# Two normalizations of a transformer block: the squares behind the second one taken as sums per 512 columns

## The chip, the cores and the metric

The program runs on one core of one Trainium2 chip. A core has TensorE (matmuls and transposes, with a separate path for its weights), VectorE, ScalarE, GpSimd (called POOL in the profile) and SyncE, whose queue issues most transfers. The metric is device time in microseconds (us) of one execution; lower is better.

## The reference, cut to what matters

Two transformer blocks in a row, for 256 rows of 2048 values, all in fp32. The first projects to attention and a gate, attends in a sliding window, projects back and adds the normalized result to x. The second has its scales, shifts and gates computed from a vector c, two attentions, an output projection and a feed-forward part. The change touches the two places where a projection ends, is normalized, is added to x, and the sum is normalized again for the next projection:

```python
def rmsnorm(x, g):
    xf = x.astype(jnp.float32)
    r = lax.rsqrt(jnp.mean(xf * xf, axis=-1, keepdims=True) + NORM_EPS)
    return (xf * r * g.astype(jnp.float32)).astype(x.dtype)
...
    y = (o * silu(z)) @ w_out            # first place
    x = x + rmsnorm(y, g_post)
    h = _rmsnorm(x, g_pre_mix) * (1.0 + sc1) + sh1
    proj = h @ w_in
...
    y = (sigmoid(ga) * ya + sigmoid(gb) * yb) @ w_o      # second place
    x = x + gt1 * _rmsnorm(y, g_post_mix)
    h = _rmsnorm(x, g_pre_ffn) * (1.0 + sc2) + sh2
    f = square(relu(h @ w_ff1)) @ w_ff2
```

## The kernel before, in words

The 256 rows are two halves t = 0 and 1 of 128 rows. A value that feeds a matmul is kept as a high part and a low remainder. A weight tile `rw` arrives by DMA, ScalarE copies its high part `wh` (L68) and VectorE takes the remainder `wl` (L69). A product is high x high, low x high (activation low) and high x low (weight low).

`unit` (L118 to L158) multiplies by 512 columns of a weight matrix, slice pair by slice pair: for each half 4 matmuls with `wh` (L75, L76) and 2 with `wl` (L78), all 512 columns wide. With `lag` the second half runs that many steps behind the first. Functions in the list `later` are called one step on. `blocks_of` (L160 to L183) computes 128 columns of a weight matrix for both halves together: 512-column matmuls with `wh` (L172), 256-column ones with `wl` (L174), by eight slices.

`project_and_norm` (L513) is called for both places. It runs four units of 512 columns, the last one with a lag of 7 steps. When a half of a unit is done, ScalarE squares it with a sum (L533) and VectorE multiplies it by the gain row (L538). Behind the last one the sums are added, POOL raises them to -1/2 (L216), VectorE forms xp = x + yn * r in four pieces (L549), ScalarE squares these (L550), the sums are added (L553), POOL gives the second factor, four pieces are scaled by it (L560, L562), TensorE transposes them (L565), ScalarE and VectorE apply scale and shift (L571, L574), and the result is split into the next operand's tiles (L195, L197), called A and B in the first place, B and D in the second.

`ada_rows` (L344) sends a row of the computed gates to HBM and back, spread over all partitions, by two transfers. It is put on a list of side work at L825. `out_b` (L838) is the last stage before the second place; its transposes go through `to_operand` (L203).

Every engine executes its own instructions in one fixed order, set when the program is built by the framework's scheduler, and waits on semaphores. SyncE's queue issues transfers in its order too, and an issue that waits holds up those behind it.

## Time and profile before

| | |
|---|---|
| time, median of 3 runs | 1794.07 us (1791.09 to 1795.02) |
| the profiled execution | 1789.49 us |
| its span | 1787.7 us |
| granted TensorE clock, mean | 0.998 |
| TensorE busy | 1769.1 us, 99% |
| VectorE busy | 1314.5 us, 74% |
| ScalarE busy | 859.6 us, 48% |
| mean DMA rate | 248 GB/s |

A timeline row gives the start, the time from there to the last end, and how many instructions it holds; the note in brackets is the idle time before the row and what ended it. Instructions of one engine overlap at their edges, so the pitch is read from the starts. Rows of one line may be joined (x8). For each of the 20 idle matmuls at the start (L236) the trace holds two records.

### The profile page before, as it was taken

What the parts mean: (1) busy time and instruction counts of PE and PEld (TensorE: products, weight loads), DVE (VectorE), ACT (ScalarE), POOL (GpSimd) and SP (SyncE); (2) the same over time, 40 slices, a digit from 0 to 9 for tenths busy, and PEclk for the clock granted to TensorE, in tenths of its full rate; (3) what the DMA queues carried; (4) which work ended last, traced back from release to release, by engine and by line L of the source; (5) the groups of instructions that cost most, each with busy time, mean ns of one, the idle gap of its engine ahead of it and who ended that gap; (6) DMA issues with size and microseconds to landing.
All of it is one profiled execution on the core that took longest, in us unless ns stands there. A gap on an engine that the chain in (4) does not pass through costs nothing.

```text
span 1787.7 us, 23509 instructions
## 1 busy us (share of the span) xinstructions
PE 1769.1 (99%) x8992; PEld 1495.5 (84%) x8992; DVE 1314.5 (74%) x1894; ACT 859.6 (48%) x1265; POOL 10.3 (1%) x16
## 2 busy tenths in 40 slices
PE   9999999999999999999999999999999999999998
PEld 8888888788888888888887878888888888888886
DVE  5998888668998897677777567767676756565656
ACT  6555454654454454444443466444344434344433
POOL 0000000000000000000000000000000000000000
PEclk9999999999999999999999999999999999999999
DMA  8887768754677775688786666766666655555552
GB/s 309 328 295 286 272 274 331 252 185 154 268 281 265 304 277 206 238 313 306 301 304 247 247 239 252 271 238 249 240 253 241 251 188 189 190 187 195 186 198 104
DMA packets 82192, 442.99 MB, mean 248 GB/s; under 512 B 9760, under 2 KB 9760, under 8 KB 43552
## 3 DMA queue, kind: packets, MB, share of 16 engines
q1 hardware_dynamic: 82080, 441.50, 67.3%
q8 instruction: 70, 1.15, 0.2%
q14 instruction: 42, 0.34, 0.1%
HBM read 435.14 MB, written 6.32 MB: 247 GB/s over the span
## 4 chain that ended last, share of the span: by engine, by line
PE 94%; DMA 2%; DVE 2%; ACT 1%; issue 0%; POOL 0%; SPq 0%; DVEq 0%; POOLq 0%; ACTq 0%
PE acc L172 22%; PE acc L75 19%; PE acc L78 18%; PE acc L76 18%; PE acc L174 11%; DMA xs<-in_x 1%; PE att L456 1%; PE tr L407 1%; PE att L764 1%; PE tr L446 1%; PE tr L724 1%; DMA rw<-in_win 0%; DMA rw<-in_wf 0%; PE tr L208 0%; PE tr L681 0%
## 5 line engine op out<-in xcount | busy, mean ns | idle before, releaser
L68 ACT ACTIVATE wh<-rw 128x1024 fp32r<-128x1024 f32 (+1 forms) x602 | 634.6, 1059 | 775.2 <-PE acc L76 473.3
L69 DVE TENSOR_TENSOR wl<-rw,wh 128x1024 fp32r<-128x1024 f32 (+1 forms) x602 | 731.4, 1220 | 341.6 <-ACT wh L68 334.6
L332 DVE SCALAR_TENSOR_TENSOR araw<-araw,aacc 128x1024 f32<-128x1024 f32 x176 | 213.8, 1218 | 52.3 <-DMA araw<-in_wada 52.0
L75 PE MATMUL acc<-wh,A 128*128 128x512 f32 x624 | 245.5, 393 | 0.4 <-ACT A L195 0.4
L76 PE MATMUL acc<-wh,A 128*128 128x512 f32 x624 | 243.4, 390 | 0.8 <-DVE A L197 0.8
L172 PE MATMUL acc<-B,wh 128*128 128x512 f32 x864 | 219.1, 395 | 0.0
L78 PE MATMUL acc<-wl,A 128*128 128x512 f32 x624 | 193.1, 390 | 0.0
L172 PEld LDWEIGHTS acc<-B,wh 128*128 128x128 f32 x864 | 155.7, 189 | 29.9 <-issue 1.3
L75 PE MATMUL acc<-wh,C 128*128 128x512 f32 x448 | 174.7, 390 | 1.6 <-ACT wh L68 1.6
L76 PE MATMUL acc<-wh,C 128*128 128x512 f32 x448 | 174.6, 390 | 0.0
L75 PEld LDWEIGHTS acc<-wh,A 128*128 128x128 f32 x624 | 117.2, 188 | 25.3 <-issue 1.0
L76 PEld LDWEIGHTS acc<-wh,A 128*128 128x128 f32 x624 | 117.3, 188 | 24.8 <-DVE A L197 1.2
L78 PEld LDWEIGHTS acc<-wl,A 128*128 128x128 f32 x624 | 117.0, 188 | 25.1 <-DVE wl L69 0.4
L78 PE MATMUL acc<-wl,C 128*128 128x512 f32 x448 | 137.9, 389 | 0.0
L75 PE MATMUL acc<-wh,B 128*128 128x512 f32 x320 | 126.3, 395 | 0.4 <-ACT B L195 0.4
L76 PE MATMUL acc<-wh,B 128*128 128x512 f32 x320 | 124.9, 390 | 0.8 <-DVE B L197 0.8
L174 PEld LDWEIGHTS acc<-B,wl 128*128 128x128 f32 x864 | 117.9, 190 | 8.5
L174 PE MATMUL acc<-B,wl 128*128 128x256 f32 x864 | 120.8, 282 | 0.0
L172 PE MATMUL acc<-D,wh 128*128 128x512 f32 x480 | 120.3, 392 | 0.0
L75 PEld LDWEIGHTS acc<-wh,C 128*128 128x128 f32 x448 | 84.1, 188 | 19.2 <-ACT wh L68 1.9
L172 PEld LDWEIGHTS acc<-D,wh 128*128 128x128 f32 x480 | 86.3, 189 | 15.4
L172 PE MATMUL acc<-A,wh 128*128 128x512 f32 x384 | 99.0, 399 | 0.0
(212 smaller groups left out, 1978.4 us busy)
## 6 DMA issues: line engine op xcount, KB each, us to landing
rw<-in_wf SPq DMA_DIRECT2D x124, 1024.0 KB, 4.8
araw<-in_wada SPq DMA_DIRECT2D x176, 512.0 KB, 5.8
rw<-in_win SPq DMA_DIRECT2D x40, 1024.0 KB, 5.5
rw<-in_wqk SPq DMA_DIRECT2D x32, 1024.0 KB, 4.8
rw<-in_wq SPq DMA_DIRECT2D x16, 1024.0 KB, 7.0
rw<-in_wout SPq DMA_DIRECT2D x16, 1024.0 KB, 5.8
rw<-in_wga SPq DMA_DIRECT2D x16, 1024.0 KB, 4.8
rw<-in_wgb SPq DMA_DIRECT2D x16, 1024.0 KB, 4.9
```

Source lines behind the costliest of these rows:

```text
L68: A.activation(wh, src, AF.Copy)
L69: V.tensor_tensor(wl, src, wh.bitcast(F32), op=ALU.subtract)
L75: PE.matmul(ps, lhs(ht, 0, k, t), wh[:, i], start=start and i == 0, stop=False)
L76: PE.matmul(ps, lhs(ht, 1, k, t), wh[:, i], start=False, stop=False)
L78: PE.matmul(ps, lhs(ht, 0, k, t), wl[:, i], start=False, stop=stop and i == len(ks) - 1)
L172: PE.matmul(ps, wh[:, kk], xs[kk].rearrange("p e t -> p (e t)"), start=first + kk == 0, stop=False)
L174: PE.matmul(ps[:, 0:T], wl[:, kk], xs[kk][:, 0], start=False, stop=first + kk == nk - 1)
L332: V.scalar_tensor_tensor(rw, rw, 0.5, cb, op0=ALU.mult, op1=ALU.mult, accum_out=cols[i][:, half, b:b + 1])
L407: PE.matmul(sps[e][:, i * nk:(i + 1) * nk], qT[64 * e:64 * e + 64, 2 * hf + i, t * 128:(t + 1) * 128], kTd[64 * e:64 * e + 64, g, 0:nk], s ...
L446: PE.transpose(tr[:, i * 128:(i + 1) * 128], s[:, h, b * 128:(b + 1) * 128], ident)
L456: PE.matmul(pos[t][:, hh * 64:(hh + 1) * 64], pT[:, i], vn[:, b, g * 64:(g + 1) * 64], start=b == 0, stop=b == nb - 1)
L724: PE.matmul(sp[:, i * nk:(i + 1) * nk], qT[:, h, t * 128:(t + 1) * 128], kT[:, h, 0:nk], start=True, stop=True)
```

## The change

- In `blocks_of` the low matmuls of all slices of a block come behind all of its high ones.
- `gpre` and the first weights are issued by ScalarE's queue, the latter in two pieces that are split one by one (`split_by_tile`). Eleven idle matmuls stand in front of the program, where 20 stood.
- `project_and_norm` takes three sums per 512 columns: of y squared, of (y times gain) squared, and of y times gain times x. x is loaded once more for it (`xq`). From them and the sum of x squared, kept in `msx`, the second factor is worked out with operations on one column; the sum x + yn * r is squared nowhere. For half 0 the four pieces of the operand are put off by 3 to 6 steps.
- The gate row of `ada_rows` is called behind `out_b`, by `soon(2, ...)`, and the last transposes of `out_b` one step later.

```diff
+    def split_by_tile(src, shape, pl):
+
+        wh = pl.tile(shape, F32R, name="wh")
+        wl = pl.tile(shape, F32R, name="wl")
+        for i in range(shape[1]):
+            A.activation(wh[:, i], src[:, i], AF.Copy)
+            V.tensor_tensor(wl[:, i], src[:, i], wh[:, i].bitcast(F32), op=ALU.subtract)
+        return wh, wl
...
+    def soon(n, f):
+
+        later.append(f if n == 0 else lambda: soon(n - 1, f))
...
-                if before:
-                    nc.sync.dma_start(rw[:, hh], src[:, hh])
+                if before and n == 0:
+                    for i in range(2):
+                        nc.scalar.dma_start(rw[:, i], src[:, i])
                     use()
-                parts.append(split(rw[:, hh], [128, 2, 512], "", split_pool()))
+                    parts.append(split_by_tile(rw[:, hh], [128, 2, 512], split_pool()))
+                else:
+                    if before:
+                        nc.sync.dma_start(rw[:, hh], src[:, hh])
+                        use()
+                    parts.append(split(rw[:, hh], [128, 2, 512], "", split_pool()))
...
+            if first == 0:
+                lows = []
             xs = [ht[(k0 + first + kk) // 8][:, (k0 + first + kk) % 8] for kk in range(8)]
             for kk in range(8):
                 PE.matmul(ps, wh[:, kk], xs[kk].rearrange("p e t -> p (e t)"), start=first + kk == 0, stop=False)
-            for kk in range(8):
-                PE.matmul(ps[:, 0:T], wl[:, kk], xs[kk][:, 0], start=False, stop=first + kk == nk - 1)
+                lows.append((wl[:, kk], xs[kk][:, 0]))
             if 8 * (hh + 1) % nk == 0:
+                for n, (wlk, xh) in enumerate(lows):
+                    PE.matmul(ps[:, 0:T], wlk, xh, start=False, stop=n == nk - 1)
...
-    for _ in range(20):
+    for _ in range(11):
...
-            nc.sync.dma_start(gpre, I["gpre"])
+
+            nc.scalar.dma_start(gpre, I["gpre"])
...
-        r = rstd(ss, f"x{t}")
+        V.tensor_scalar(msx[t], ss, 1.0 / D, EPS, op0=ALU.mult, op1=ALU.add)
+        r = power(msx[t], f"x{t}")
...
-            ssy = [pst.tile([128, 4], F32, name=f"ssy{t}") for t in range(2)]
+            sums = [pst.tile([128, 3, 4], F32, name=f"sums{t}") for t in range(2)]
+            tot = [pst.tile([128, 3], F32, name=f"tot{t}") for t in range(2)]
...
                     cc = slice(j * 512, (j + 1) * 512)
-                    A.activation(yn[t][:, cc], ps, AF.Square, accum_out=ssy[t][:, j:j + 1])
+                    sm = sums[t]
+                    xq = px.tile([128, 512], F32, name="xq", bufs=1)
+                    nc.sync.dma_start(xq, xsrc[t * 128:(t + 1) * 128, cc])
+                    A.activation(yn[t][:, cc], ps, AF.Square, accum_out=sm[:, 0, j:j + 1])
+                    V.tensor_tensor(yn[t][:, cc], ps, grow[:, cc], op=ALU.mult)
+                    A.activation(ps, yn[t][:, cc], AF.Square, accum_out=sm[:, 2, j:j + 1])
                     if j == 3:
-                        ss = pst.tile([128, 1], F32, name="ss")
-                        V.tensor_reduce(ss, ssy[t], axis=AX.X, op=ALU.add)
-                        r = rstd(ss, "y")
-                    V.tensor_tensor(yn[t][:, cc], ps, grow[:, cc], op=ALU.mult)
+
+                        m = pst.tile([128, 3], F32, name="m3")
+                        V.scalar_tensor_tensor(m[:, 0:1], sm[:, 0, 3:4], 1.0 / D, tot[t][:, 0:1], op0=ALU.mult,
+                                               op1=ALU.add)
+                        r = power(m[:, 0:1], "y")
+                    V.scalar_tensor_tensor(xq, yn[t][:, cc], 2.0, xq, op0=ALU.mult, op1=ALU.mult,
+                                           accum_out=sm[:, 1, j:j + 1])
+                    if j == 2:
+                        V.tensor_reduce(tot[t], sm[:, :, 0:3], axis=AX.X, op=ALU.add)
+                        V.tensor_scalar(tot[t], tot[t], 1.0 / D, None, op0=ALU.mult)
+                        V.tensor_scalar(tot[t][:, 0:1], tot[t][:, 0:1], EPS, None, op0=ALU.add)
                     if j == 3:
-                        finish(t, r)
-
-                def finish(t, r):
+                        V.scalar_tensor_tensor(m[:, 1:3], sm[:, 1:3, 3], 1.0 / D, tot[t][:, 1:3], op0=ALU.mult,
+                                               op1=ALU.add)
+                        V.scalar_tensor_tensor(m[:, 1:2], m[:, 2:3], r, m[:, 1:2], op0=ALU.mult, op1=ALU.add)
+                        V.scalar_tensor_tensor(msx[t], m[:, 1:2], r, msx[t], op0=ALU.mult, op1=ALU.add)
+                        V.tensor_scalar(msx[t], msx[t], EPS, None, op0=ALU.max)
+                        finish(t, r, power(msx[t], "h"))
+
+                def finish(t, r, r2):
                     rows = slice(t * 128, (t + 1) * 128)
-                    ss2 = pst.tile([128, 4], F32, name="ss2")
-                    for c in range(4):
+
+                    def operand(c):
                         cc = slice(c * 512, (c + 1) * 512)
-                        xp = px.tile([128, 512], F32, name="xp", bufs=4)
+                        xp = px.tile([128, 512], F32, name="xp", bufs=3)
                         nc.sync.dma_start(xp, xsrc[rows, cc])
-                        V.scalar_tensor_tensor(xp, yn[t][:, cc], r, xp, op0=ALU.mult, op1=ALU.add)
-                        A.activation(yn[t][:, cc], xp, AF.Square, accum_out=ss2[:, c:c + 1])
-                        xps.append(xp)
-                    ss = pst.tile([128, 1], F32, name="ss")
-                    V.tensor_reduce(ss, ss2, axis=AX.X, op=ALU.add)
-                    r = rstd(ss, "h")
-                    for c in range(4):
-                        xp = xps.pop(0)
-                        nc.sync.dma_start(xdst[rows, c * 512:(c + 1) * 512], xp)
-                        xn = yn[t][:, c * 512:(c + 1) * 512]
-                        if c == 3:
-                            A.activation(xn, xp, AF.Copy, scale=r)
+                        V.scalar_tensor_tensor(yn[t][:, cc], yn[t][:, cc], r, xp, op0=ALU.mult, op1=ALU.add)
+                        nc.sync.dma_start(xdst[rows, cc], yn[t][:, cc])
+                        xn = xp
+                        if c % 2:
+                            A.activation(xn, yn[t][:, cc], AF.Copy, scale=r2)
                         else:
-                            V.tensor_scalar(xn, xp, r, None, op0=ALU.mult)
+                            V.tensor_scalar(xn, yn[t][:, cc], r2, None, op0=ALU.mult)
...
+                    for c in range(4):
+                        if t == 0:
+                            soon(3 + c, lambda c=c: operand(c))
+                        else:
+                            operand(c)
...
-        side.append(ada_rows(2, gg1, first[:, 624:640], first[:, 640:656]))
...
-                later.append(lambda: to_operand(mT, 4 * j, t, o, 0.5))
+                soon(1 if j == 3 else 0, lambda: to_operand(mT, 4 * j, t, o, 0.5))
...
+        soon(2, lambda: drain([ada_rows(2, gg1, first[:, 624:640], first[:, 640:656])]))
```

On VectorE, behind the last Square of half 0 in the first place, before (`yr` and `hr` are the two factors, `xp` the pieces of the sum, `wl` the low parts of weights):

```order
330 L536 TENSOR_REDUCE ss<-ssy_2572 128x1
331 L538 TENSOR_TENSOR yn_2570<-acc,gpost 128x512
332 L215 TENSOR_SCALAR yv<-ss 128x1
333 L549 SCALAR_TENSOR_TENSOR xp<-yn_2570,yr,xp 128x512 x4
334 L69 TENSOR_TENSOR wl<-rw,wh 128x1024 x2
335 L553 TENSOR_REDUCE ss<-ss_3151 128x1
336 L215 TENSOR_SCALAR hv<-ss 128x1
337 L69 TENSOR_TENSOR wl<-rw,wh 128x1024
338 L562 TENSOR_SCALAR yn_2570<-xp,hr 128x512 x3
```

The same place now (`xq` is the extra load of x, `m` and `msx` one-column values):

```order
341 L594 SCALAR_TENSOR_TENSOR yn_2564<-yn_2564,yr,xp 128x512
342 L573 SCALAR_TENSOR_TENSOR xq,sums_2566<-yn_2564,xq 128x512
343 L594 SCALAR_TENSOR_TENSOR yn_2564<-yn_2564,yr,xp 128x512
344 L580 SCALAR_TENSOR_TENSOR m_3174<-sums_2566,tot_2568 128x2
345 L594 SCALAR_TENSOR_TENSOR yn_2564<-yn_2564,yr,xp 128x512
346 L582 SCALAR_TENSOR_TENSOR m_3174<-m_3174,yr 128x1
347 L69 TENSOR_TENSOR wl<-rw,wh 128x1024
348 L583 SCALAR_TENSOR_TENSOR msx_88<-m_3174,yr,msx_88 128x1
349 L69 TENSOR_TENSOR wl<-rw,wh 128x1024
350 L584 TENSOR_SCALAR msx_88<-msx_88 128x1
351 L69 TENSOR_TENSOR wl<-rw,wh 128x1024
352 L600 TENSOR_SCALAR xp<-yn_2564,hr 128x512 x2
```

The four pieces and a sum stood in front of two splits; now three pieces, the xy product and four small steps stand among three splits.

On TensorE, the transposes of half 0 in the first place and what follows them up to the next unit, before:

```order
859 L565 MATMUL tr<-first,yn_2570 128x128 x12
860 L75 MATMUL acc<-wh,D 128x512
861 L76 MATMUL acc<-wh,D 128x512
862 L78 MATMUL acc<-wl,D 128x512 x2
863 L75 MATMUL acc<-wh,D 128x512
864 L76 MATMUL acc<-wh,D 128x512
865 L75 MATMUL acc<-wh,D 128x512
866 L76 MATMUL acc<-wh,D 128x512
867 L78 MATMUL acc<-wl,D 128x512
868 L565 MATMUL tr<-first,yn_2570 128x128 x4
869 L78 MATMUL acc<-wl,D 128x512
870 L75 MATMUL acc<-wh,A 128x512
```

The same now (from the transposes to the next unit):

```order
857 L603 MATMUL tr<-first,xp 128x128 x8
858 L84 MATMUL acc<-wh,D 128x512
859 L85 MATMUL acc<-wh,D 128x512
860 L87 MATMUL acc<-wl,D 128x512 x2
861 L603 MATMUL tr<-first,xp 128x128 x4
862 L84 MATMUL acc<-wh,D 128x512
863 L85 MATMUL acc<-wh,D 128x512
864 L84 MATMUL acc<-wh,D 128x512
865 L85 MATMUL acc<-wh,D 128x512
866 L87 MATMUL acc<-wl,D 128x512 x2
867 L84 MATMUL acc<-wh,A 128x512
```

Eight transposes instead of twelve come first, and the four of the last piece no longer stand ahead of the next unit; in both orders 38 of the 48 matmuls of half 1 stand between half 0's last one and these transposes. Half 1's first transposes stand 40 matmuls into the next unit before, and 33 now.

On SyncE's queue, the gate row (`row`, `gg`) and the first weights of the second place (`in_wo`), before:

```order
283 L331 DMA araw<-in_wada 128x1024 x5
284 L352 DMA row_8443<-cols_323 128x16
285 L353 DMA gg_6801<-row_8443 128x2048
286 L135 DMA rw<-in_wo 128x2048 x8
287 L548 DMA xp<-xsave 128x512 x2
```

And now:

```order
291 L355 DMA araw<-in_wada 128x1024 x5
292 L376 DMA row_8548<-cols_319 128x16
293 L377 DMA gg_6821<-row_8548 128x2048
294 L144 DMA rw<-in_wo 128x2048 x4
295 L563 DMA xq<-xsave 128x512
```

The row stands where it stood, ahead of all weights of wo; the first load of `xq` has come behind the first four of these.

## Rows read from the trace of the kernel before

**Rows 1.** The page's line of engines: busy us, share of the span, instructions.
```profile
## 1 busy us (share of the span) xinstructions
PE 1769.1 (99%) x8992; PEld 1495.5 (84%) x8992; DVE 1314.5 (74%) x1894; ACT 859.6 (48%) x1265; POOL 10.3 (1%) x16
```

**Rows 2.** Waits of TensorE: us in total, times, longest us.
```profile
PE tr L565 <- DVE yn L562: 2.6, 4, 1.1
PE acc L75 <- ACT wh L68: 1.6, 1, 1.6
...
PE tr L208 <- DVE rw L849: 1.0, 2, 0.7
PE acc L76 <- DVE A L197: 0.8, 1, 0.8
PE acc L76 <- DVE B L197: 0.8, 1, 0.8
PE acc L75 <- ACT A L195: 0.4, 1, 0.4
PE acc L75 <- ACT B L195: 0.4, 1, 0.4
```

**Rows 3.** Timeline of TensorE, first blocks of ff1: start us, length, instruction, count.
```profile
1094.91 1.98 PE L172 MATMUL acc<-B,wh 128*128 128x512 f32 x8
1096.73 1.11 PE L174 MATMUL acc<-B,wl 128*128 128x256 f32 x8
...
1100.92 2.00 PE L172 MATMUL acc<-B,wh 128*128 128x512 f32 x8
1102.76 1.12 PE L174 MATMUL acc<-B,wl 128*128 128x256 f32 x8
```

**Rows 4.** Windows (busy by engine, then PEclk, DMA share, GB/s) and timeline, the start.
```profile
1.00:6.00 5.00, 4.92 (x23) 4.92 (x24) 0.91 (x3) 2.12 (x4) 0.00 (x0) 1.00 0.70 180
6.00:8.00 2.00, 2.00 (x16) 2.00 (x16) 0.00 (x0) 0.96 (x1) 0.00 (x0) 1.00 0.94 319
...
7.04 1.06 ACT L68 ACTIVATE wh<-rw 128x1024 fp32r<-128x1024 f32 x1 [2.29 <-DMA rw<-in_win]
...
8.28 0.48 PE L75 MATMUL acc<-wh,A 128*128 128x512 f32 x1
...
12.31 1.06 ACT L68 ACTIVATE wh<-rw 128x1024 fp32r<-128x1024 f32 x1 [0.34 <-DMA rw<-in_win]
...
14.12 0.39 PE L75 MATMUL acc<-wh,A 128*128 128x512 f32 x1
```

**Rows 5.** Timeline of TensorE, from out_b to the first matmul of wo.
```profile
975.42 0.63 PE L208 MATMUL tr<-first,rw 128*128 128x128 f32 x4 [0.73 <-DVE rw L849]
977.68 0.50 PE L75 MATMUL acc<-wh,C 128*128 128x512 f32 x1 [1.63 <-ACT wh L68]
```

**Rows 6.** Timeline of ScalarE, POOL, VectorE and TensorE, first place, half 0.
```profile
339.41 0.60 ACT L533 ACTIVATE yn<-acc 128x512 f32<-128x512 f32 x1 [4.49 <-PE acc L78]
...
341.02 0.55 POOL L216 TENSOR_TENSOR yr<-yv,mhalf 128x1 f32<-128x1 f32 x1 [293.14 <-DVE yv L215]
346.95 1.48 POOL L216 TENSOR_TENSOR hr<-hv,mhalf 128x1 f32<-128x1 f32 x1 [5.38 <-DVE hv L215]
...
341.61 2.74 DVE L549 SCALAR_TENSOR_TENSOR xp<-yn,yr,xp 128x512 f32<-128x512 f32 x4 [0.66 <-POOL yr L216]
344.27 2.35 DVE L69 TENSOR_TENSOR wl<-rw,wh 128x1024 fp32r<-128x1024 f32 x2
...
346.80 1.23 DVE L69 TENSOR_TENSOR wl<-rw,wh 128x1024 fp32r<-128x1024 f32 x1
348.47 1.28 DVE L562 TENSOR_SCALAR yn<-xp,hr 128x512 f32<-128x512 f32 x3 [0.44 <-POOL hr L216]
...
349.01 1.53 PE L565 MATMUL tr<-first,yn 128*128 128x128 f32 x12 [0.94 <-DVE yn L562]
...
355.08 0.50 PE L76 MATMUL acc<-wh,A 128*128 128x512 f32 x1 [0.85 <-DVE A L197]
```

**Rows 7.** Timeline of TensorE, first place, half 1.
```profile
364.53 1.53 PE L565 MATMUL tr<-first,yn 128*128 128x128 f32 x12 [0.24 <-DVE yn L562]
```

**Rows 8.** Timeline of TensorE, second place, half 0.
```profile
1064.07 1.50 PE L565 MATMUL tr<-first,yn 128*128 128x128 f32 x12 [1.10 <-DVE yn L562]
```

More of the change, by code (lines that the diff above doesn't have):

```diff
@@ L88, in step @@
                 gens.pop(0)
-    def flush():
-        while later:
-            later.pop(0)()
+    def soon(n, f):
+        later.append(f if n == 0 else lambda: soon(n - 1, f))
     def drain(gens):
@@ L213, in rstd, with power @@
         v = pst.tile([128, 1], F32, name=name + "v")
+        V.tensor_scalar(v, ss, 1.0 / D, EPS, op0=ALU.mult, op1=ALU.add)
+        return power(v, name)
+    def power(v, name):
         r = pst.tile([128, 1], F32, name=name + "r")
-        V.tensor_scalar(v, ss, 1.0 / D, EPS, op0=ALU.mult, op1=ALU.add)
         G.tensor_tensor(r, v, mhalf, op=ALU.pow)
@@ L232, in _build @@
     gpre = pc.tile([128, KT], F32, name="gpre")
+    msx = [pc.tile([128, 1], F32, name=f"msx{t}") for t in range(2)]
     idle = bank(patt, "att")
-    for _ in range(20):
+    for _ in range(11):
         PE.matmul(idle[:, 0:128], ones, ones, start=True, stop=True)
@@ L576, in finish @@
                         evict_split(out, 4 * c, t, tmp, 4)
-                xps = []
+                    for c in range(4):
[3 more added lines that the diff above has]
+                            operand(c)
                 unit(w, j, ht, done, lag=LAG if j == 3 else 0, rate=0.67 if first and j < 3 else 0.0)
```

## The prediction

> **What bounds the kernel now.** I read the page's engine line first [rows 1]: TensorE has work in flight for 1769.1 of the 1787.7 us span, 99%, and no other engine passes 84%. So a change can move the end only by changing how many matmul columns pass or how close they stand, or by opening or closing TensorE's gaps. Second, the waits of TensorE [rows 2]: the longest kinds are its waits in front of the transposes of the second normalization (2.6 us over the four chains, two halves in each of two places), the evictions behind them (0.8 + 0.8 + 0.4 + 0.4), and one place around out_b (1.0 and 1.6). The reader is to see how little there is: the normalizations hold 5.0 us of idle time and the out_b place 2.6, with some 0.2 us more lost at each restart. Third, the timelines of those stretches, engine by engine, walked by hand below. Sums are made against the profiled execution (1789.49 us, span 1787.7); it lies 4.6 us under the median of the three runs, 1794.07, and the difference found is carried over to that median.
>
> **Pass order.** 108 blocks have 16 weight slices. Before, each does 8 high matmuls, 8 low, 8 high, 8 low; now 16 high and then 16 low. The work is the same; only the change from 256-column to 512-column matmuls becomes rarer. Eight high matmuls take 1.82 us to the next instruction where a 512-column matmul stands in front (1094.91 to 1096.73) and 1.84 where a low one does (1100.92 to 1102.76) [rows 3]. So one such change fewer is worth about 0.02 us per block, 108 x 0.018 = 1.9 us: **-1.9 us**, between 0 and -3. The low weights are held one half longer, but nothing waits for those buffers in [rows 2].
>
> **First transfers.** The gpre columns and the first weights (now two pieces) are issued by ScalarE's queue instead of SyncE's, the split works by piece, and 11 idle matmuls stand in front instead of 20. Before, the idle ones run without a break until the first weights are split (7.04 + 1.06 = 8.10) and the first real matmul starts at 8.28 [rows 4]. The piecewise split can bring that forward by about half a split, 0.5 us. But the third pair of slices is split at 12.31 + 1.06 = 13.37 and wanted at 14.12: a start more than 0.75 us earlier only meets that transfer. I take **-0.4 us**. Bounds: -1.5 if the later transfers come forward too; +1.5 if TensorE's clock is low when the real work starts. For the idle records run at two paces, 23 in the 5 us before 6.0 and 16 in the 2 us behind (granted clock shown as 1.00 in both), so 11 instructions, 22 records, end near 5.9 and leave a gap of 1 to 2 us that was not there.
> The Trainium skill (DMA: Bandwidth & Descriptors, Issuing engines are not separate DMA queues) says that transfers from several engines end up on the same 16 DMA engines and only the issuing time is saved. The DMA share of 0.70 and 0.94 in those two stretches does not contradict it; by that rule the first weights, issued later than before and sharing with the second pair, would land no sooner, and the term would be 0.
>
> **Gate row.** The source now calls the row's assembly after out_b and puts the last transposes one step later. On SyncE's queue the two row transfers still stand ahead of the first weights of wo, and on TensorE the eight transposes still stand in one piece ahead of the first matmul of wo. The 1.63 us wait for that first split stays [rows 5]: **0 us**; bounds 0 and -2.6 (the idle time there).
>
> **The second normalization.** Per 512 columns and half there is one more transfer of 256 KB, one more Square on ScalarE and one more product with a sum on VectorE. For the first three of the four column groups they lie beside a TensorE that does not wait for them. VectorE is 74% busy and ScalarE 48% [rows 1]. I cost them at nothing; without that cover they would be 12 times some 0.7 us on VectorE. What counts is the last group, where the chain from the last Square to the transposes is on the path.
> Before, with T = 339.41, the start of the last Square of half 0 in the first place [rows 6]: the first xp product starts at T + 2.20 behind POOL's power, the four take 2.66, two weight splits and the sums follow, a third split starts at T + 7.39, and POOL's second power runs beside it from T + 7.54 to T + 9.02. The scale starts at T + 9.06, the transposes at T + 9.60 after a wait of 0.94, and the second matmul of the next unit at T + 15.67.
> Now, walked in VectorE's new order: product at T + 2.1; then two xp products, the xy product and a third xp product, 4 x 0.665 = 2.66, with two one-column operations of 0.15, to T + 5.1; then a split of 1.17, a one-column step of 0.17, a second split, a second step: T + 7.8. The power starts at T + 8.0, again beside a split, and takes 1.48: T + 9.5, and the scale begins at **T + 9.7**, 0.6 us later than before, not earlier. The four Squares and the sum that left the chain paid for themselves before by lying on ScalarE beside the two splits; in their place stand two short steps, each behind a whole split.
> TensorE has the same 38 matmuls to cover this as before, so it arrives at the same T + 8.45 and waits 1.8 us instead of 1.1 (idle 0.94 and the restart). Then comes the eviction of the next operand: same work, starting later, with only three of the four transposed groups of half 0 done; the next unit starts near T + 16.1 with a second stall of 2.0 (before: 0.4 + 0.85 and two restarts, 1.8). For half 1 I see more loss. Before, 40 matmuls of the next unit stand between the start and its transposes, which then wait only 0.24 [rows 7]; now 33 do, 1.6 us less cover, while its scale comes only some 0.6 us sooner: a stall of 1.1. Three matmuls behind it comes half 1's operand, which has to be evicted first: 1.6; and 0.4 at the last group. Together 1.8 + 2.0 + 1.1 + 1.6 + 0.4 = 6.9 against 1.1 + 1.8 + 0.3 = 3.2: **+3.7 us**.
> The second place is walked the same way: there the first wait is 1.10 [rows 8], the sum before 3.3 and after 6.9, **+3.6 us**. I give each place 1.5 us either way; the ends are -3.2 (no wait left) and +6.
> POOL's power takes 0.55 us where VectorE rests and 1.48 beside a weight split [rows 6]. If the second power met a resting VectorE, each of the first two stalls would be 0.9 shorter, and the time 1797.3; I take 1.48, since a split stands right behind the last one-column step in the new order too.
> The Trainium skill (SBUF — State Buffer, SBUF: two separate sides) says why the order decides it: a VectorE instruction with two SBUF inputs and a GpSimd one that reads SBUF lock each other out for their whole length, whichever starts first. By that rule a power that starts ahead of the split would take 0.55 and hold the split up instead; the trace of before shows only the other case, 1.48.
>
> **Sum.** -1.9 - 0.4 + 0 + 3.7 + 3.6 = +5.0 us: 1794.5 for the profiled execution, 1794.07 + 5.0 = **1799.1** against the median.
>
> **Rivals.**
> *The chain gets shorter, as the source has it.* Four Squares (some 2.5 us) are gone from it; the one-column steps may slip in while splits wait for their high parts, and only two scaled groups are needed before transposes begin. For: splits on VectorE do wait for ScalarE in other stretches, since every split stands behind its high part. Against: three splits stand in the new order inside the chain. If the idle time of both places shrinks by half, -3, the sum is -1.9 - 0.4 - 3 = -5.3, 1788.8. It decides where the second power starts before T + 6.5. This is the case on the faster side. Chance 0.19.
> *The normalizations come out as before.* The lost cover and the shorter chain cancel: only pass order and start count, -2.3, 1791.8. For: the waits of before are short, and TensorE does the same work between the same two ends. Chance 0.24.
> *The start loses.* In the gap behind 11 idle matmuls TensorE falls back to the pace that it had in the first 5 us, 0.217 against 0.125 us a record [rows 4]; some 20 real matmuls that take 1.7 times as long (0.40 instead of 0.23) cost 3.4 us, of which the wait for the third pair hides about half, on top of the forecast: 1801. Chance 0.09.
> *The gate row does move*, and the 2.6 us go: with the forecast elsewhere 1796.5, no change. Chance 0.03.
> The forecast has 0.45.
>
> **How the numbers follow.** About 0.2%, 3.6 us, is what a measurement can tell from no change: 1790.5 to 1797.7. Faster: the first rival, and a small part of the second, 0.21. The same: most of the second, the fourth and the low end of the forecast (1.5 us either way at each place), 0.31. Slower: the rest of the forecast and the third, 0.48. The forecast's own range is 1796 to 1802; with the second rival and the edge of the first, and the start's +1.5, the range is 1789 to 1802.5.
>
> **What would show it.** Right: in the profile after, TensorE's idle time ahead of the first transposes of each normalization near 1.6, four stalls in each instead of three, and a second power that starts about 8 us behind the last Square beside a weight split. Pass order: two halves of a block 5.57 us apart instead of 5.58. Gate row: still a wait of 1.6 ahead of wo. Start: first real matmul near 7.8, the third pair at about 14. Wrong: a power that ends under 8 us behind the Square, or transposes that wait less than 0.5 us, sends it to the first rival; matmuls 0.4 us apart in the first 12 us, to the third.

## The result, and the profile after

The changed kernel takes 1801.69 us (median of 4 runs, 1801.30 to 1804.87), the kernel before 1793.30 on the same chip (4 runs): the ratio is 1.0051 with a 95% interval of 1.0038 to 1.0064, so it is slower by about 9 us. The forecast was slower, by 5.0, at 1799.1.

The profiled execution took 1801.44 us and its span is 1799.7, 12.0 more than the one of before. That pair lies further apart than the medians, 8.4. The page of the changed kernel, its line of engines (busy us, share, instructions), against [rows 1]:

```profile
PE 1772.8 (99%) x8974; PEld 1496.5 (83%) x8974; DVE 1326.0 (74%) x1939; ACT 868.4 (48%) x1270; POOL 10.3 (1%) x16
```

VectorE and ScalarE have 12 and 9 us more work, and neither is short of time: the loss must be gaps of TensorE or a slower pace. Its waits, the same view as [rows 2] (us in total, times, longest us):

```profile
PE tr L603 <- DVE xp L600: 4.8, 3, 3.1
PE acc L84 <- ACT wh L77: 1.9, 2, 1.5
PE acc L87 <- DVE wl L69: 1.9, 2, 1.5
PE acc L84 <- ACT A L213: 1.7, 2, 0.9
PE acc L84 <- ACT wh L68: 1.6, 1, 1.6
PE acc L84 <- ACT B L213: 1.6, 1, 1.6
...
PE acc L85 <- DVE A L215: 1.1, 2, 0.8
PE tr L226 <- DVE rw L892: 1.0, 2, 0.7
PE tr L226 <- DVE cols L373: 0.7, 1, 0.7
PE tr L226 <- DVE mix L892: 0.4, 1, 0.4
PE acc L85 <- DVE B L215: 0.2, 1, 0.2
```

The waits at the second normalization's transposes went from 2.6 to 4.8 with one of 3.1, the evictions behind them from 2.4 to 4.6 (L213 and L215 together), and new are the waits for the first weights (L77), for a low part of weights (L69) and, around out_b, for `cols` and `mix` (1.1 together). L226 <- rw and L84 <- wh L68, around the gate row, read as before.

To see where the time goes, each instruction of TensorE is paired with the same one of before, and the start times are subtracted. The difference, by the time in the kernel before, with those of the experiments told of below:

```
us later than before at  100    325    345    384    450    480    700    970   1050   1165   1775
changed kernel           1.2    1.2    1.9    5.5    6.1    7.8    7.7    9.2   10.7   12.9   12.0
pass order alone         0.5    0.6    0.6    0.6    0.7    2.5    2.3    7.8    7.8    7.6    6.7
first transfers alone    1.7    2.4    2.4    2.4    2.4    2.5    2.5    2.5    2.5    2.5    2.5
normalization alone      0.0    0.3    5.9   12.7   13.2   13.2   13.3   14.1   16.9   18.0   18.0
gate row alone          -0.4   -0.4   -0.4   -0.4   -0.3   -0.3   -0.3    7.8    9.4    9.5    9.5
```

The steps of the first row: start 1.2, first place 4.9 (325 to 450), index stage 1.7 (450 to 480), at the transposes of out_b 1.5 (700 to 970), a low pace behind the gate row 1.5 (970 to 1050), second place 2.2 (1050 to 1165), and the feed-forward blocks behind it give 0.9. Not all of these belong to the change: the gate row alone left every engine's order as it was, and yet it lost 8.1 us between 700 and 970, from nothing but the scatter of one execution to the next. 30 executions of the kernel before on one chip ran from 1789.4 to 1800.7 us. So a step behind 700 us in one trace alone is not yet put down to the change; steps ahead of it are read from the traces.

The start of the changed kernel, TensorE's timeline (start, length, instruction, count, idle before), against [rows 4]:

```profile
1.08 5.06 PE L259 MATMUL att<-ones 128*128 128x128 f32 x22 [1.08 <-DVE ones L249]
7.63 0.80 PE L84 MATMUL acc<-wh,A 128*128 128x512 f32 x1 [1.48 <-ACT wh L77]
...
9.73 0.80 PE L84 MATMUL acc<-wh,A 128*128 128x512 f32 x1 [0.46 <-ACT wh L77]
...
11.61 0.63 PE L85 MATMUL acc<-wh,A 128*128 128x512 f32 x1
12.03 0.63 PE L84 MATMUL acc<-wh,A 128*128 128x512 f32 x1
```

The first real matmul starts 0.65 us sooner than the 8.28 of before, but its fellows stand 0.42 us apart (11.61 to 12.03) up to 13.7, and the second piece of the weights is late: ScalarE splits it at 9.05. At 20 us TensorE is 2.4 us late; half of that comes back at 48 us, where the kernel before itself waits 1.00 us for ScalarE (`qn`) and the changed one does not.

The first place: the gain product of the kernel before, which [rows 6] leaves out, then ScalarE and VectorE of the changed kernel, the same view:

```profile
340.21 0.68 DVE L538 TENSOR_TENSOR yn<-acc,gpost 128x512 f32<-128x512 f32 x1
```

```profile
341.29 0.60 ACT L564 ACTIVATE yn<-acc 128x512 f32<-128x512 f32 x1 [3.00 <-PE acc L87]
```

```profile
340.71 1.23 DVE L356 SCALAR_TENSOR_TENSOR A<-A 128x1024 f32<-128x1024 f32 x1 [0.49 <-DMA A<-in_wada]
...
342.33 1.22 DVE L356 SCALAR_TENSOR_TENSOR A<-A 128x1024 f32<-128x1024 f32 x1
...
344.13 0.68 DVE L565 TENSOR_TENSOR yn<-acc,gpost 128x512 f32<-128x512 f32 x1
...
345.55 0.75 DVE L594 SCALAR_TENSOR_TENSOR yn<-yn,yr,xp 128x512 f32<-128x512 f32 x1 [0.66 <-POOL yr L237]
...
352.48 0.88 DVE L600 TENSOR_SCALAR xp<-yn,hr 128x512 f32<-128x512 f32 x2 [0.44 <-POOL hr L237]
```

The last Square starts at T = 341.29. The gain product starts at T + 2.84, where it was T + 0.8 in before: two column sums of the scales (L356) and what hangs on them stand ahead of it. From there to the scaling it takes 8.35 us (344.13 to 352.48), just what it took before, 8.26 from the gain product at 340.21 to 348.47. The scale begins at T + 11.2; I had said T + 9.7. What put the column sums there is on SyncE's queue, the changed kernel's timeline (start of the issue, its length):

```profile
335.14 0.33 SPq L563 DMA_DIRECT2D xq<-in_x  x1
335.51 0.90 SPq L355 DMA_DIRECT2D A<-in_wada  x2
336.51 0.38 SPq L144 DMA_DIRECT2D rw<-in_win  x1
340.25 0.33 SPq L563 DMA_DIRECT2D xq<-in_x  x1
```

`xq` has one buffer. The load at 335.14 could be issued only when the product of the group before had read the buffer (to 335.1), and the one at 340.25 likewise (340.2). The last weights of the column sums and those of the next unit stood behind it in the queue's order; in before the last of these column weights were issued at 304 us.

The second place, TensorE of the changed kernel, against [rows 8]:

```profile
1073.41 0.63 PE L603 MATMUL tr<-first,xp 128*128 128x128 f32 x4 [1.14 <-DVE xp L600]
...
1087.51 1.53 PE L603 MATMUL tr<-first,xp 128*128 128x128 f32 x12 [0.63 <-DVE xp L600]
1090.63 0.49 PE L84 MATMUL acc<-wh,B 128*128 128x512 f32 x1 [1.59 <-ACT B L213]
1091.36 0.50 PE L85 MATMUL acc<-wh,B 128*128 128x512 f32 x1 [0.23 <-DVE B L215]
```

There half 0 waits as before (1.14 against 1.10) and no longer for its operand; half 1 waits 0.63 + 1.59 + 0.23, where it had 0.33.

### The profile page after: what moved, and what is told of

Its sections match the earlier page's. It is cut to its first block, busy times and chain, and to the rows that moved or that the text cites. A ratio compares the mean times of both kernels' runs of the same rounds, so it can differ in the third digit from the quotient of the medians.

```text
span 1799.7 us, 23545 instructions
## 1 busy us (share of the span) xinstructions
PE 1772.8 (99%) x8974; PEld 1496.5 (83%) x8974; DVE 1326.0 (74%) x1939; ACT 868.4 (48%) x1270; POOL 10.3 (1%) x16
## 4 chain that ended last, share of the span: by engine, by line
PE 92%; DVE 5%; DMA 1%; ACT 1%; issue 1%; POOL 0%; DVEq 0%; POOLq 0%; ACTq 0%; SPq 0%
PE acc L189 21%; PE acc L84 18%; PE acc L85 18%; PE acc L87 18%; PE acc L193 11%; DVE wl L69 1%; PE att L481 1%; DMA rw<-in_win 1%; PE tr L432 1%; DVE sc L736 1%; PE att L808 1%; PE tr L471 1%; PE tr L768 1%; PE tr L226 0%; ACT wh L68 0%
## 5 line engine op out<-in xcount | busy, mean ns | idle before, releaser
L68 ACT ACTIVATE wh<-rw 128x1024 fp32r<-128x1024 f32 (+1 forms) x601 | 633.7, 1058 | 684.3 <-PE acc L85 455.4
L69 DVE TENSOR_TENSOR wl<-rw,wh 128x1024 fp32r<-128x1024 f32 (+1 forms) x601 | 725.8, 1222 | 298.5 <-ACT wh L68 232.3
L84 PE MATMUL acc<-wh,A 128*128 128x512 f32 x624 | 247.2, 396 | 3.6 <-ACT wh L77 1.9
L356 DVE SCALAR_TENSOR_TENSOR araw<-araw,aacc 128x1024 f32<-128x1024 f32 x176 | 213.7, 1220 | 36.3 <-DMA araw<-in_wada 36.0
L84 PE MATMUL acc<-wh,C 128*128 128x512 f32 x448 | 175.5, 392 | 1.6 <-ACT wh L68 1.6
L84 PEld LDWEIGHTS acc<-wh,A 128*128 128x128 f32 x624 | 117.9, 189 | 30.0 <-ACT wh L77 3.0
L84 PE MATMUL acc<-wh,B 128*128 128x512 f32 x320 | 127.1, 397 | 1.6 <-ACT B L213 1.6
L189 PEld LDWEIGHTS acc<-D,wh 128*128 128x128 f32 x480 | 90.1, 188 | 18.6
L84 PEld LDWEIGHTS acc<-wh,C 128*128 128x128 f32 x448 | 84.5, 189 | 19.3 <-ACT wh L68 1.9
L87 PE MATMUL acc<-wl,B 128*128 128x512 f32 x320 | 99.3, 392 | 0.0
```

The source lines that it names most:

```text
L68: A.activation(wh, src, AF.Copy)
L69: V.tensor_tensor(wl, src, wh.bitcast(F32), op=ALU.subtract)
L84: PE.matmul(ps, lhs(ht, 0, k, t), wh[:, i], start=start and i == 0, stop=False)
L87: PE.matmul(ps, lhs(ht, 0, k, t), wl[:, i], start=False, stop=stop and i == len(ks) - 1)
L189: PE.matmul(ps, wh[:, kk], xs[kk].rearrange("p e t -> p (e t)"), start=first + kk == 0, stop=False)
L356: V.scalar_tensor_tensor(rw, rw, 0.5, cb, op0=ALU.mult, op1=ALU.mult, accum_out=cols[i][:, half, b:b + 1])
```

## The experiments

Twelve kernels, each built from the kernel before. A ratio is to runs of the kernel before on the same chip, with its 95% interval.

**Pass order alone.** The edit of `blocks_of` in the diff above, nothing else.

> Before with the pass order alone (all 16 high matmuls of a block, then all 16 low). Theory A, read from the two traces: the blocks save 0.26 us over the first 16, some 0.4 over the next 32 and 1.1 over the last 60, 1.7 in all, but the scheduler, which plans VectorE's order anew, puts one weight split behind the key rotation of the index stage (L786) instead of ahead of it, and TensorE waits 1.7 us for it near 470 us, as in the changed kernel: 1793.3 - 1.7 + 1.7 = 1793.3, within 1 us of before, and the trace shows that one wait. Rival B, my forecast's term: the saving alone, 1791.4, with no such wait.

1.0006 (0.9993 to 1.0019). Theory A; rival B's 1791.4 us would be 0.9988, outside the interval. The new wait is there, one of TensorE's waits in that kernel:

```profile
PE acc L78 <- DVE wl L69: 1.5, 1, 1.5
```

By the table it costs 1.8 us (450 to 480), and the 60 last blocks give 1.1 (1050 to 1775). The order on VectorE shows the cause: before, the weight split stands ahead of the chain of `rb`, `rl` and `kT` in the index stage, with pass order alone behind it:

```profile
465.97 1.21 DVE L69 TENSOR_TENSOR wl<-rw,wh 128x1024 fp32r<-128x1024 f32 x1
...
471.55 0.68 DVE L783 TENSOR_TENSOR kT<-rl,rb 128x512 f32<-128x512 f32 x1
```

```profile
471.11 0.68 DVE L786 TENSOR_TENSOR kT<-rl,rb 128x512 f32<-128x512 f32 x1
...
472.10 1.22 DVE L69 TENSOR_TENSOR wl<-rw,wh 128x1024 fp32r<-128x1024 f32 x1
```

In the changed kernel too: `kT` at 476.43 and the split at 477.42, with TensorE waiting.

**First transfers alone**, and **the same with 20 idle matmuls**:

```diff
-    for _ in range(11):
+    for _ in range(20):
```

> Before with the new first transfers and 11 idle matmuls alone. Theory A: the matmuls from 7.6 to 13.7 us run 0.43 us apart instead of 0.23, and the sequence behind them is 1.5 us late, as in the changed kernel: 1794.8. Rival B, my forecast's term: the start is 0.4 us sooner, 1792.9, and what the changed kernel loses there comes from elsewhere.

> Before with the new first transfers, but 20 idle matmuls as before. Theory A (the start loses by TensorE's pace, not by the transfers): the idle ones bridge the time to the first weights, the real matmuls stand 0.23 us apart from the start, and the sequence at 50 us is at most 0.5 us later than before, where with 11 idle ones it was 2 us later: 1793.7. Rival B (the transfers themselves came later, since the second piece of the first weights lands behind the second pair): still 2 us later, 1795.

1.0006 (0.9993 to 1.0019) with 11 and 0.9999 (0.9983 to 1.0015) with 20: no time can tell them from before or from each other, so the trace has to speak. At 100 us they are 1.7 and 1.6 us late. So rival B: 20 idle matmuls do not mend it. Their kernel's timeline:

```profile
8.44 0.50 PE L84 MATMUL acc<-wh,A 128*128 128x512 f32 x1 [1.04 <-ACT wh L77]
8.78 0.40 PE L85 MATMUL acc<-wh,A 128*128 128x512 f32 x1
10.15 0.50 PE L84 MATMUL acc<-wh,A 128*128 128x512 f32 x1 [0.98 <-ACT wh L77]
...
11.58 0.63 PE L85 MATMUL acc<-wh,A 128*128 128x512 f32 x1
12.01 0.63 PE L84 MATMUL acc<-wh,A 128*128 128x512 f32 x1
```

TensorE starts at the high pace (0.34 us from 8.44, with the first one's restart in it) and waits again for the second piece, which puts it 1.3 us behind before; the pace falls at 11.2, behind these two waits of 1 us, and costs 1.5 us more, until at 48 us some 1.2 come back as above. So the transfers lose time without any help of the pace; that the waits bring the pace down is what the order of the two suggests, no run separates them. The Trainium skill (DMA: Bandwidth & Descriptors, Issuing engines are not separate DMA queues) says that transfers which several engines start run on the same 16 DMA engines, and that only the time of the issue is saved. The trace agrees: the first weights are split at 7.04 in before, their two pieces at 6.95 and 9.05 in the changed kernel and at 7.77 and 9.47 with 20 idle matmuls.

**Gate row alone.**

> Before with the gate row behind out_b and the later last transposes alone. The program's instructions stand in the order of before on every engine, so any theory expects 1793.3 us, 0 within 0.2%. What differs between the two traces is then what one and the same program does from one execution to the next: by theory A the waits at 972 to 974 us and the low clock behind 987 us, 2.9 us in the changed kernel's trace, may show here too, by rival B (these belong to the change) never.

1.0004 (0.9989 to 1.0019), with the same order of instructions on every engine: the part does nothing. Its profile holds a wait that the one of before does not have, on VectorE and then on TensorE:

```profile
873.82 1.23 DVE L332 SCALAR_TENSOR_TENSOR araw<-araw,aacc 128x1024 f32<-128x1024 f32 x1 [6.24 <-DMA araw<-in_wada]
```

```profile
878.79 0.63 PE L208 MATMUL tr<-first,mix 128*128 128x128 f32 x4 [3.21 <-DVE mix L848]
```

A late transfer of the side work (issued at 863.72, landed at 873.72; the one before it took 6.3 us) stops VectorE for 6.2 us, and a product of the main work stands behind it; TensorE then runs at a granted clock of 0.50 from 881 to 886 us. So the waits at 970 us and the low pace behind 985, 3.0 us of the 12.0 between the profiled executions, are of a kind that the program of before shows by itself (rival B falls); whether the change makes them more frequent these runs can't tell.

**Normalization alone.**

> Before with the three sums and the deferred operand alone (the second normalization). Theory A: the first place loses 4.7 us (VectorE's column sums of the scales, whose last weights land late, stand ahead of the last gain product, so that the whole chain starts 2 us late and TensorE waits 3 us at the transposes), the second place 1 us in waits, and 1.8 more if TensorE's clock falls behind them: 1793.3 + 5.7 to 7.5 = 1799 to 1801, with the wait of 3 us in the trace. Rival B, my forecast: 3.7 and 3.6 us, 1800.6, with waits of 1.8 at the transposes in both places and no late start of the chain.

1.0038 (1.0019 to 1.0057), 1801.06 us: by the medians nearly the whole loss of the changed kernel. In its profile, of the slowest of its seven executions (1807.38 us), the loss is larger, and begins sooner than theory A has it, in front of the last unit: 5.6 us between 325 and 345. ScalarE and VectorE of that kernel:

```profile
333.45 1.06 ACT L68 ACTIVATE wh<-rw 128x1024 fp32r<-128x1024 f32 x1 [3.81 <-DMA rw<-in_wout]
```

```profile
318.00 0.69 DVE L553 SCALAR_TENSOR_TENSOR xq<-yn,xq 128x512 f32<-128x512 f32 x1 [2.42 <-DMA xq<-in_x]
```

It is the single buffer again, by another way. The load of `xq` is issued at 311.58, when its buffer is free, and lands at 317.90; a load of the projection's own weights stands behind it in the queue (312.00, where before has 305.82). VectorE waits 2.42 us for `xq` ahead of two weight splits, and the next loads of weights wait for buffers that the splits free: they are issued at 321.00 and 325.70, where before has 316.71 and 322.14, and the last one lands at 333.43 instead of 326.91.

**Column sums earlier; no deferral; xq on another queue.** Three edits of the normalization alone, one each (`...` stands for arguments left as they are):

```diff
-                unit(..., rate=0.67 if first and j < 3 else 0.0)
+                unit(..., rate=0.8 if first and j < 3 else 0.0)
```
```diff
-                        if t == 0:
-                            soon(3 + c, lambda c=c: operand(c))
-                        else:
-                            operand(c)
+                        operand(c)
```
```diff
-                    nc.sync.dma_start(xq, ...)
+                    nc.scalar.dma_start(xq, ...)
```

> The kernel with the normalization change alone, its side work in the first place (the last columns of the scales) paced at 0.8 instead of 0.67. By the order of its instructions the column sums are then done before the last gain product of half 0, and the chain behind that product has two weight splits in it instead of three. Theory A (the first place loses because these column sums, whose weights land late, stand ahead of the chain): the wait at the first transposes there falls from 1.8 to 3 us to under 1, the place loses 2 us or less instead of 4 to 7, and the time is 1797. Rival B (the lost cover behind half 1 and the evictions decide, as in my forecast): 1800, with the waits in front of half 1's operand unchanged.

> The kernel with the normalization change alone, but the pieces of half 0's operand are not put off. By its order twelve transposes come first again, as in before, and the fourth piece comes ahead of the next unit. Theory A (late column sums and the queue): the wait at the first transposes stays near 3, since the chain ahead of it is the same, and the time stays within 2 us of the 1800 of the normalization alone. Rival B (the deferral lost the cover): half 1's operand no longer waits, 1.5 us in each place come back, 1797.

> The kernel with the normalization change alone, the extra load of x (xq) issued by ScalarE's queue instead of SyncE's. Theory A (xq has one buffer, its issue waits for the product of the group before, and the weights of the scales and of the next units stand behind it on SyncE's queue): with xq off that queue the last weights of the scales are issued near 304 to 310 us as in before, not at 335, the splits do not wait for weights, and the first place loses 2 us or less: 1796 to 1797. It can lose on ScalarE, where the issue now waits in front of weight splits: each such wait over 1 us would show as a wait of TensorE for wh. Rival B (the chain itself, not the queue): 1800.

1.0041 (1.0027 to 1.0056), 1.0042 (1.0026 to 1.0058) and 1.0058 (1.0040 to 1.0075): none helps, the last is if anything worse. Theory A falls in the first: the column sums are out of the way, and the wait at the transposes is longer, 4.3 us. VectorE and TensorE of that kernel:

```profile
345.76 0.69 DVE L553 SCALAR_TENSOR_TENSOR xq<-yn,xq 128x512 f32<-128x512 f32 x1 [2.24 <-DMA xq<-in_x]
```

```profile
352.09 1.12 PE L583 MATMUL tr<-first,xp 128*128 128x128 f32 x4 [4.29 <-DVE xp L580]
```

Behind the column sums had hidden what now comes first: the x of the last group is issued when its buffer is free (341.27), lands 4.4 us later, and VectorE waits 2.24 us for it in the middle of the chain. On ScalarE's queue it is the same, 2.37 us: the queue is not what makes this load late, the single buffer is. There the last column weights are issued at 304 to 307 us again, as in before, so it was `xq` on SyncE's queue that had moved them; but that alone gives no time back. Without the deferral the waits for half 1's operand are gone, as rival B has it, but half 1's transposes in the second place wait 2.43 us, and 6.6 us go between 325 and 345 us as in the profile of the normalization alone.

**One ring of four buffers.**

```diff
-                    xq = px.tile([128, 512], F32, name="xq", bufs=1)
+                    xq = px.tile([128, 512], F32, name="xp", bufs=4)
...
-                        xp = px.tile([128, 512], F32, name="xp", bufs=3)
+                        xp = px.tile([128, 512], F32, name="xp", bufs=4)
```

> The kernel with the normalization change alone, but the extra load of x takes its buffer from the four that the pieces xp had before (one ring of 4, instead of 1 for xq and 3 for xp). Theory C, formed from the two runs before: xq has one buffer, so the last group's x is issued only behind the product of the group before, some 4.5 us late, and VectorE waits 2.2 to 2.4 us for it in the middle of the chain; the weights of the scales stand behind that issue as well. With the ring this wait is gone, the wait at the first transposes of the first place falls from 3 to 4.3 us to about 1, and the place loses 2 to 3 us (what half 1's operand costs) instead of 4.7 to 7: 1797. Rival B (the order of the chain): still 1800.

1.0030 (1.0012 to 1.0048), 1797.83 us, as theory C has it; its interval and that of the normalization alone overlap, but the traces do not: between 325 and 450 us this kernel loses 2.5 us, the normalization alone 12.9 and the other four profiles with a single buffer 4.9 to 10.1. The order of VectorE has the column sums ahead of the chain by itself now. What is left there is half 1: 2.5 us at its transposes and a wait of 0.8 behind them.

**The ring, side work at 0.8, no deferral.** The last edit with the first two of the three above.

> The same with one ring of 4, side work paced at 0.8, and half 0's pieces not put off. By its order twelve transposes come first in both places, and half 1's stand as deep in the next unit as in before. Theory C: no wait for x, no column sums in the chain, and the cover of half 1 is back; each place waits no more than before, 2.5 us: 1793 to 1794, the same as before. Rival B (three pieces, the xy product and the small steps are no shorter than four pieces and a sum): 1.5 us more in each place, 1797.

0.9997 (0.9982 to 1.0013), 1792.51 us: the whole loss is gone. The interval lies apart from that of no deferral with the single buffer (1.0026 to 1.0058), and the side work's pace alone had given nothing (1.0041), so times as well as traces show what the buffer costs. The same extra loads of x are made here, so their bytes cost nothing that can be measured. The chain of half 0 in the first place, VectorE, and TensorE:

```profile
339.95 0.69 DVE L545 TENSOR_TENSOR yn<-acc,gpost 128x512 f32<-128x512 f32 x1 [4.65 <-ACT yn L544]
...
346.53 0.89 DVE L580 TENSOR_SCALAR xp<-yn,hr 128x512 f32<-128x512 f32 x2 [0.44 <-POOL hr L219]
```

```profile
347.07 1.53 PE L583 MATMUL tr<-first,xp 128*128 128x128 f32 x12 [1.05 <-DVE xp L580]
...
363.31 1.53 PE L583 MATMUL tr<-first,xp 128*128 128x128 f32 x12 [0.30 <-DVE xp L580]
```

From the gain product to the scaling it is 6.6 us, where before had 8.3: here the sums do shorten the chain, by 1.7. TensorE still waits 1.05 at the first transposes, since in this order it comes there sooner, but the first place as a whole gains 0.5 (325 to 450 us in a table like the one above), the second 0.4.

**Pass order in the feed-forward blocks alone**, and **this with the last normalization**:

```diff
-        blocks_of(I["wf1"], b - 4, hF, [done], rate=rate)
+        blocks_of(I["wf1"], b - 4, hF, [done], rate=rate, late=True)
```

> Before with the new pass order in the 60 blocks of the feed-forward part alone. Theory A: these save 18 ns each, 1.1 us, and the index stage keeps its order on VectorE, so that no split comes late there: 1792.5, and the trace shows two blocks 11.14 instead of 11.17 us. Rival: the saving is eaten by a wait for wl as in the index stage: 1793.6.

> The two parts that did not lose, together: the normalization with one ring of 4, side work at 0.8 and no deferral, and the new pass order in the feed-forward blocks alone; first transfers, gate row and the other blocks as in before. Theory A, from the two traces: the first place gives 0.6 us, the blocks 1.1, 1.7 together: 1791.5, 0.1% faster than before, near the limit of what is measurable. Rival: what the two give is within the scatter from one execution to the next, and the scheduler's new order costs as much elsewhere: 1793.

0.9989 (0.9973 to 1.0004) and 0.9991 (0.9976 to 1.0005): both on the side of faster, neither clear of no change. By the traces, paired as above, the blocks give 1.1 us in both (the first is 9.9 us late at 1050 and 8.8 at the end, the second 2.0 at 1098 and 0.8), and no weight split comes late in the index stage. A version that beats the kernel before by more than its scatter was not found.

## Why the prediction was right in sign, and which steps were not

The forecast was slower by way of the two normalizations, and that is where the loss is: the normalization alone gives 0.38% of the 0.51%. Step by step:

- **Pass order, -1.9.** The saving of a block is right: two half blocks of high matmuls take 3.66 us and two of low ones 1.91 in the changed kernel, 5.57 a block, as forecast:

```profile
1114.05 2.00 PE L189 MATMUL acc<-B,wh 128*128 128x512 f32 x8
...
1117.71 1.11 PE L193 MATMUL acc<-B,wl 128*128 128x256 f32 x8
...
1119.62 2.00 PE L189 MATMUL acc<-B,wh 128*128 128x512 f32 x8
```

  The net is not: the scheduler moved a split elsewhere, and 1.7 us were lost in the index stage. I had said that nothing waits for the low weights; I looked at their buffers and not at the order of VectorE in the other stages.
- **First transfers, -0.4.** Wrong: 1.2 us lost in the changed kernel, 1.7 alone. The third rival's sign is there, matmuls 0.42 us apart, but it had the cause in the gap behind 11 idle matmuls, and with 20 the loss is the same: the second piece, split at 9.05, is what the forecast had left out. The first piece was issued sooner than the whole before (1.23 against 1.65), not later as I had it, and still gained only 0.1.
- **Gate row, 0.** Right: no instruction moves.
- **The cost of the sums "at nothing" ahead of the last group.** This is the step that failed. The work itself hides, as I said. But I counted a transfer of 256 KB and forgot to ask what its issue waits for: one buffer, which is free only behind the product of the group before. That wait holds SyncE's queue, and with it the column weights (first place 2 us); or it holds VectorE's splits and so the projection's own weights (5.6 and 6.6 us in two profiles); or, if neither, the chain itself (2.2 to 2.4 us).
- **The chain of half 0, T + 9.7.** Wrong in both places. In the first it is T + 11.2: the first xp product starts at T + 4.3, behind the column sums, where I had T + 2.1, and from there to the scaling it takes 6.9 us, where I had 7.6. In the second place, where no column sums stand in it and x lands in time, the changed kernel scales at 1072.78, T + 7.8 with T = 1065.02, where before has T + 9.1 and I had carried over 9.7; its second power starts at T + 6.4, the first rival's sign. TensorE is idle for 3.05 us ahead of the first transposes in the first place and 1.14 in the second; I had named 1.6 for both. With the load in time the chain of the first place is shorter too, as the first rival had it: from the gain product to the scaling 7.0 us with the ring alone (two splits in it) and 6.6 without the deferral (one), where before has 8.3 with three. So the forecast's main claim, that the squares had paid for themselves, falls.
- **Half 1, 1.1 + 1.6 + 0.4.** The mechanism was right: with the deferral fewer matmuls cover its chain. The changed kernel shows 0, 0.89 and 0.23 idle in the first place, 0.63, 1.59 and 0.23 in the second; with the ring alone it is what remains, and with the ring and without the deferral it is 0.9 and 0.8 in all.
- **The two places together, +7.3.** The normalization alone measures +7.5 (1801.06 against 1793.56; by the interval 3.4 to 10.2). That the sums agree is luck: the changed kernel's trace has 4.9 in the first place, with a late start of the chain that the forecast does not have, and 2.2 in the second, where I had 3.6: its waits grew by 0.9, most of the rest being a low pace behind them.
- **POOL's power.** 1.46 us beside a split again in the changed kernel (350.98), 0.55 where VectorE rests, and 0.99 with the ring, side work at 0.8 and no deferral (345.50), where an xp product of 0.75 us that began at 345.34 is under way. The two that found a VectorE instruction under way end 0.40 us behind its end. The rule of the Trainium skill (SBUF — State Buffer, SBUF: two separate sides) that I weighed, whoever starts first holds the other off, fits all three; no run here shows a power that holds a VectorE instruction up.

## What to carry to other kernels

Of a load that is added, ask first which buffer its issue waits for, and then who stands behind that issue in the queue; its bytes may cost nothing while its wait costs several us elsewhere. A shorter chain gains nothing if its cover is shortened too: more buffers alone gave back a part of the loss by the traces, the deferral's undoing alone nothing, both together, with the side work's pace at 0.8, all of it. Whether that pace is needed beside the two was not run; alone it gave nothing. A pass order that saves 18 ns a block can move a split in a stage that no line of the edit touches; compare the order on the helper engines everywhere, not only at the edit.

## What the runs showed of the hardware that was not expected

TensorE's pace falls in the middle of the program, behind gaps of few us, and only in some executions. Windows of the changed kernel (busy time of each engine, then the granted clock, DMA share, GB/s):

```profile
986.90:990.20 3.30, 3.29 (x8) 2.62 (x9) 3.30 (x3) 2.83 (x4) 0.00 (x0) 0.52 0.72 298
992.00:995.00 3.00, 3.00 (x15) 2.50 (x14) 1.80 (x2) 0.95 (x2) 0.00 (x0) 1.00 0.89 300
1092.40:1095.70 3.30, 3.30 (x9) 2.54 (x8) 2.34 (x4) 1.70 (x4) 0.00 (x0) 0.51 0.17 63
8.00:13.70 5.70, 5.24 (x12) 3.64 (x12) 4.03 (x7) 4.65 (x9) 0.00 (x0) 1.00 1.04 399
```

Behind the gate row (waits of 0.24, 0.73 and 1.63) and behind half 1's operand in the second place (0.63, 1.59, 0.23) the clock is 0.52 and 0.51, that is 1.2 GHz, for 3.3 us, which costs some 1.6 us each. The same three waits at the gate row left it at full pace in the profile of before, and brought it down in that of the gate row alone, the same program. At the start the pace is just as low and the granted clock reads 1.00: there the pitch of the matmuls tells it (0.42 us, where [rows 3] have 0.23), not the clock.
